# Retention in steps, GpSimd's own stores, SWA's first operands and a new start in an encoder layer

## The chip, the cores and the metric

The kernel runs on one core of a Trainium2 chip. The metric is the device time of one launch in microseconds (us), lower is better. Engines are named as in the profile: PE is TensorE, PEld its weight loads, DVE VectorE, ACT ScalarE, POOL GpSimd, and SP issues most of the transfers. A difference of 0.2% is 4.5 us here.

## The reference

One inference step of a one-layer encoder on 1024 prompt tokens and 64 sample tokens, D_MODEL 1024, all in 32-bit floats. One wide projection gives retention's q, k, v and gate, the queries, keys and values of sliding-window attention (SWA), and two branch gates:

```python
xn = rms_norm(x, g_attn)
rq, rk, rv, rg, sq, sk, sv, ga, gb = split(xn @ w_in)
# A: retention, 4 heads of 256, chunks of 64
q = rope(rq); k = rope(rk) / 16
s = einsum('bihd,bjhd->bhij', q, k) * gamma ** abs(i - j)
o = s @ v + (q @ state) * q_dec
state = state * gamma ** C + (k * k_dec).T @ v
a = (rms_norm(o) * silu(rg)) @ w_ret_out
# B: SWA, 16 heads of 64 on 2 kv heads, window 128, bias by relative position, sinks
p = softmax(sq @ sk.T / 8 + rel_bias, with sinks)
b = (p @ sv) @ w_swa_out
x = x + (sigmoid(ga) * a + sigmoid(gb) * b) @ w_mix_out
x = x + cross_attn(rms_norm(x), memory)      # 4 heads, 256 memory tokens
x = x + (silu(hn @ w_gate) * (hn @ w_up)) @ w_down
return rms_norm(x), states, keys, values
```

The sample part runs the same layer on 64 tokens with cached state, keys and values.

## The kernel before

All 1088 tokens lie along the free axis, in halves of 544. A large product is a Strassen product: one weight matrix of 256 by 1024 is cut into quarters, the sums of quarters P1 to P7 meet the operands B11, T1, T2, B21, T3, B22, T4 and B12, formed once from the tokens. `product` makes one of the seven, `multiply` (L206, L207, L209) issues its 24 matmuls of 128x272 into a PSUM tile `pq`: each 32-bit value is a high and a low part, and three products of parts are added. `split` (L123, L124) makes the parts, the cast on ACT and the remainder on DVE; the sums of weight quarters (L184 to L190) are on POOL. `mm3` (L150 to L152) does the same three-part product for the smaller matmuls. The PSUM results of a Strassen product are combined on DVE (L571) into tiles of a small ring called `stage`, and what is made of them is stored to DRAM.

The order of instructions on each engine comes from a scheduler, which simulates a timeline and takes ready instructions; `tc.high_priority`, `tc.issue_after(x)` and `in_order` steer it.

The stages, by the trace: a start with a first product done in the plain way (`self.plain`) up to 49 us; projections and retention up to about 600; gates and memory to 823; SWA with other products between its steps (`filler`) to about 1035; then merging, cross attention and the feed-forward part, which the change does not touch.

In the start, x is loaded into staging tiles `xr`, multiplied by the gain into `xg` on ACT (L437), and split into operands.

In the projection stage, each head's k, q and v are projected; k and q are rotated with a cosine and sine table `cs`, loaded anew for each half (L603 to L608, the last two additions on POOL), and stored to `d_qkv`. The scheduler mixes the instructions of `retention(h)` among those of the next products. Retention takes blocks of 256 tokens: it loads ks, vf and qs, transposes (`turned`, L702, tile `pk`), computes scores `pss`, the state's update `pkv` and the output `po`; then `ret_out` normalizes `po` into `ret_o` (L816 to L822), turns it by four transposes into `pb` (L826), and stores it. After the four blocks comes the 64-token sample with tiles `psss`, `pos` and `pkvs`.

SWA's queries are stored to `d_sq` in pieces of 256 bytes; the relative bias is read from a table `d_rb` with a stride. SWA's filler first finishes the memory values (`pd` with `wq`, L150; its evictions are L1101), then multiplies retention's result by `w_ret_out` (`ret`, `pd`), whose first operands are loaded from `d_gate` into tiles `swin`, one feature block at a time.

Of the kernel before, what the change touches and what calls it, by code (L numbers as in the profile page):

```python
# [19 lines left out]
P = 128  # L20
# [21 lines left out]
HC = HALF // 2  # L42
OPS = ("B11", "T1", "T2", "B21", "T3", "B22", "T4", "B12")
# [66 lines left out]
class Kernel:  # L110
    def __init__(self, nc, tc, io, decay):
        self.nc, self.tc, self.io, self.decay = nc, tc, io, decay
        self.later = []
        self.refill = None

# [6 lines left out]
    def split(self, src, hi, lo):  # L122
        self.last_cast = self.nc.scalar.copy(hi, src).ins  # L123
        self.nc.vector.tensor_tensor(out=lo, in0=src, in1=hi.bitcast(F32), op=ALU.subtract)  # L124
# [42 lines left out]
    def weight_ops(self, raws, n=512, skip=()):  # L167
# [13 lines left out]
        tt = nc.gpsimd.tensor_tensor  # L181
# [8 lines left out]
        tt(out=a12, in0=a12, in1=a11, op=sub)  # L190
# [21 lines left out]
    def product(self, w, x, name, operand):  # L212
        ps = self.multiply(self.bank_pair(), w[name], x[operand])
# [131 lines left out]
    def run(self):  # L345
        nc, tc, io = self.nc, self.tc, self.io
        with ExitStack() as ctx:
# [27 lines left out]
            self.d_rb = dp.tile([16, 64 * 256], F32, name="d_rb")  # L375

# [4 lines left out]
            with ExitStack() as sctx:  # L381
# [6 lines left out]
                with tc.tile_pool(name="sixth", bufs=1, reuse_waits="tile") as sixth:  # L388
                    self.places = self.places + [sixth]
                    with self.plain_psum(2):  # L390
                        self.mix_phase()
# [23 lines left out]
    def start_phase(self, ctx):  # L415
# [9 lines left out]
        xr = lambda: sp.tile([P, HALF], F32, tag="xr", bufs=4, name="xr")  # L425
        raws = [self.wp.tile([P, 1024], F32, tag="raw", bufs=2, name="raw") for i in range(2)]

        def columns(j):
            for i in range(2):
                self.load(raws[i][:, j * 512:(j + 1) * 512].rearrange("p (k m) -> p k m", m=P), io["w_v"][i][:, 4 * j:4 * j + 4])  # L430

        def pieces(k0, t):
            hs = slice(t * HALF, (t + 1) * HALF)
            for k in range(k0, k0 + 4):
                x = xr()
                self.load(x, io["xT"][k, :, hs])
                nc.scalar.mul(self.xg[k][:, hs], x, g[:, k:k + 1])  # L437

        for n, (k0, t) in enumerate(((0, 0), (0, 1), (4, 0), (4, 1))):
            pieces(k0, t)  # L440
            if n < 2:
                columns(n)
            if n == 1:
                self.operands_early()
        self.load(self.ident, io["c_ident"])
        w = self.plain_weights(raws)
        self.operands_late()
        self.first_sums()
        self.late_sums()
# [15 lines left out]
    def token_roots(self):  # L465
# [4 lines left out]
        for i in range(9):  # L470
            w = P if i < 8 else SMP
            nc.tensor.matmul(pv[:w, i, :], self.rstd[:, i * P:i * P + w], self.ones[:, :2], start=True, stop=True)
# [1219 lines left out]
```

## Time and profile before

| what | value |
|---|---|
| three runs | 2243.85, 2244.88, 2248.97 us; median 2244.88 |
| profiled execution, its time | 2245.5 us |
| its span in the trace | 2243.7 us |
| mean granted clock of TensorE | 0.989 |

The span is what the trace records of that execution; the time beside it is the one measured from outside. In a row of the timeline stand the start, the duration, the engine and line, the operation and its tiles, and in brackets the idle time before it with what ended it. In a row of waits stand the engine and line that waited, what it waited for, and the total, count and longest in us. In a row of instruction groups, after the count, stand the total busy time and the mean of one in ns, then the idle time before. In a row of transfers stand the count, the size and the median time from issue to landing.

### The profile page before, as it was taken

How to read it: one execution, taken by the hardware profiler on the slowest of the kernel's cores; microseconds unless marked ns; L12 is line 12 of the kernel's file. 1: busy time of each engine (PE TensorE's matmuls, PEld its weight loads, DVE VectorE, ACT ScalarE, POOL GpSimd, SP SyncE). 2: the span in 40 equal slices, each digit the busy share in tenths (PEclk: the TensorE clock that was granted, in tenths of full speed). 3: DMA queues.
4: the chain of work that ended last, by engine and by line, in shares of the span. 5: the costliest groups of instructions: out<-in, count | busy, mean ns of one | idle time of the engine just before them, and what ended most of it. 6: DMA issues, size and time to landing. Idle time of an engine off the chain costs nothing.

```text
span 2243.7 us, 42075 instructions
## 1 busy us (share of the span) xinstructions
PE 2164.6 (96%) x16580; PEld 2114.4 (94%) x16580; DVE 1603.1 (71%) x2675; ACT 883.8 (39%) x1902; POOL 703.2 (31%) x471
## 2 busy tenths in 40 slices
PE   7999999999999999999999999999999999999987
PEld 7999998999999987888999998999999999999987
DVE  8986877777687667885455455658777776879777
ACT  7343333345444355554133334333322222335433
POOL 1441533242244112220000000015555565534561
PEclk9999999999999999999999999999999999999999
DMA  5644545443444576326443111422343333376332
GB/s 192 187 134 135 142 138 151 128 137 112 151 145 161 156 227 206 113 82 200 135 153 106 59 48 57 139 88 83 112 140 104 102 107 103 124 248 201 120 119 81
DMA packets 186008, 298.92 MB, mean 133 GB/s; under 512 B 40498, under 2 KB 110034, under 8 KB 185810
## 3 DMA queue, kind: packets, MB, share of 16 engines
q1 hardware_dynamic: 181458, 287.31, 40.9%
q10 hardware_dynamic: 4032, 7.80, 0.9%
q8 instruction: 131, 2.15, 0.4%
q0 software_dynamic: 320, 1.11, 0.1%
q14 instruction: 67, 0.55, 0.1%
HBM read 205.00 MB, written 91.16 MB: 132 GB/s over the span
## 4 chain that ended last, share of the span: by engine, by line
PE 70%; DVE 14%; DMA 7%; issue 3%; POOL 3%; ACT 3%; SPq 0%; POOLq 0%; DVEq 0%; ACTq 0%
PE pq L206 12%; PE pq L209 12%; PE pq L207 12%; PE pd L150 7%; PE pd L152 7%; PE pd L151 7%; DVE wq L124 3%; DVE T L124 1%; DVE B L124 1%; DMA raw<-w_down 1%; PE pss L943 1%; DMA cs<-c_rope 1%; ACT wq L123 1%; DMA hl<-d_op 1%; PE pout L1009 1%
## 5 line engine op out<-in xcount | busy, mean ns | idle before, releaser
L124 DVE TENSOR_TENSOR wq<-raw,wq 128x512 fp32r<-128x512 f32 (+1 forms) x509 | 462.1, 912 | 158.8 <-ACT wq L123 156.6
L123 ACT CAST wq<-raw 128x512 fp32r<-128x512 f32 (+1 forms) x509 | 308.0, 613 | 553.4 <-PE pq L209 206.5
L206 PE MATMUL pq<-T,wq 128*128 128x272 f32 x1832 | 502.8, 292 | 6.8 <-ACT wq L123 5.8
L207 PE MATMUL pq<-T,wq 128*128 128x272 f32 x1832 | 499.0, 289 | 0.0
L206 PE MATMUL pq<-B,wq 128*128 128x272 f32 x1574 | 433.3, 293 | 10.3 <-ACT wq L123 10.2
L207 PE MATMUL pq<-B,wq 128*128 128x272 f32 x1574 | 431.3, 290 | 4.2 <-DVE B L124 4.1
L209 PE MATMUL pq<-T,wq 128*128 128x272 f32 x1832 | 383.3, 289 | 2.5 <-DVE wq L124 2.4
L184 POOL TENSOR_TENSOR raw<-raw 128x512 f32<-128x512 f32 (+1 forms) x59 | 80.8, 1370 | 897.1 <-DVE rs_r L302 487.0
L206 PEld LDWEIGHTS pq<-T,wq 128*128 128x128 f32 x1832 | 346.8, 189 | 8.1 <-ACT wq L123 6.7
L207 PEld LDWEIGHTS pq<-T,wq 128*128 128x128 f32 x1832 | 350.0, 191 | 0.3 <-issue 0.3
L209 PE MATMUL pq<-B,wq 128*128 128x272 f32 x1574 | 329.6, 289 | 0.0
L206 PEld LDWEIGHTS pq<-B,wq 128*128 128x128 f32 x1574 | 298.8, 190 | 11.0 <-ACT wq L123 10.2
L207 PEld LDWEIGHTS pq<-B,wq 128*128 128x128 f32 x1574 | 302.0, 192 | 5.7 <-DVE B L124 5.3
L209 PEld LDWEIGHTS pq<-T,wq 128*128 128x128 f32 x1832 | 286.2, 189 | 3.8 <-DVE wq L124 2.9
L209 PEld LDWEIGHTS pq<-B,wq 128*128 128x128 f32 x1574 | 246.8, 190 | 0.5 <-issue 0.3
L263 DVE TENSOR_TENSOR u<-pq,u 128x544 f32<-128x544 f32 x177 | 127.1, 719 | 76.6 <-PE pq L209 75.9
L187 POOL TENSOR_TENSOR raw<-raw 128x512 f32<-128x512 f32 (+1 forms) x59 | 85.7, 1452 | 120.0 <-DVE wq L124 120.0
L571 DVE TENSOR_TENSOR stage<-pq,u 128x544 f32<-128x544 f32 x112 | 80.3, 717 | 26.0 <-PE pq L209 25.8
L190 POOL TENSOR_TENSOR raw<-raw 128x512 f32<-128x512 f32 (+1 forms) x59 | 90.2, 1529 | 16.0 <-DVE wq L124 12.2
L971 POOL TENSOR_TENSOR t<-t,den 128x768 f32<-128x768 f32 (+2 forms) x34 | 47.6, 1401 | 134.3 <-DVE den L969 56.7
L185 POOL TENSOR_TENSOR raw<-raw 128x512 f32<-128x512 f32 (+1 forms) x59 | 85.5, 1449 | 3.8
L1474 POOL TENSOR_TENSOR y<-u,y 128x544 f32<-128x544 f32 x38 | 61.3, 1628 | 49.3 <-DVE y L1472 24.5
(366 smaller groups left out, 4695.6 us busy)
## 6 DMA issues: line engine op xcount, KB each, us to landing
hl<-d_op SPq DMA_DIRECT2D x84, 272.0 KB, 4.1
d_qkv<-stage SPq DMA_DIRECT2D x44, 272.0 KB, 4.5
d_op<-stage SPq DMA_DIRECT2D x44, 272.0 KB, 2.5
d_op<-ht SPq DMA_DIRECT2D x44, 272.0 KB, 3.8
raw<-w_gate SPq DMA_DIRECT2D x22, 512.0 KB, 3.5
raw<-w_up SPq DMA_DIRECT2D x22, 512.0 KB, 4.2
cs<-c_rope SPq DMA_DIRECT2D x16, 544.0 KB, 4.3
raw<-w_down SPq DMA_DIRECT2D x16, 512.0 KB, 3.9
```

What stands on the lines that cost most here:

```text
L123: self.last_cast = self.nc.scalar.copy(hi, src).ins
L124: self.nc.vector.tensor_tensor(out=lo, in0=src, in1=hi.bitcast(F32), op=ALU.subtract)
L150: mm(ps, wh, xh, start=start, stop=False)
L151: mm(ps, wh, xl, start=False, stop=False)
L152: self.last_mm = mm(ps, wl, xh, start=False, stop=stop).ins
L185: tt(out=a21, in0=a21, in1=a22, op=add)
L187: tt(out=a11, in0=a22, in1=a11, op=sub)
L190: tt(out=a12, in0=a12, in1=a11, op=sub)
L206: mm(ps[:, c, :HC], w[:, 0, ks], x[:, 0, cs], start=start, stop=False)
L207: mm(ps[:, c, :HC], w[:, 0, ks], x[:, 1, cs], start=False, stop=False)
L209: self.last_mm = mm(ps[:, c, :HC], w[:, 1, ks], x[:, 0, c * HC:(c + 1) * HC], start=False, stop=stop).ins
L263: add = lambda out, a, b: nc.vector.tensor_tensor(out=out, in0=a, in1=b, op=ALU.add)
```

## The change

Four pieces of code change together.

1. Start. Twenty matmuls of constants (`WARM`) are put first on PE, and the ACT table is loaded on a constant. x is loaded straight into `xg`; the gain is multiplied into the operands while they are split, high part on ACT and low part on DVE (`put`). The first w_k's sums go to DVE, and the order of T2, T1, T3, T4 is fixed.
2. Retention is written as a generator. After each Strassen product `product` runs one step of it, and PE takes both in program order. Head h's steps run in the products after its own; loads of a block come a step ahead; `ret_out` is cut into `ret_scaled` and `ret_turn`. Head 3's steps run beside the keys, the last queries and three gate products. The rope table is one tile loaded once, and the rope additions of heads 0 and 1 are on DVE.
3. GpSimd issues the stores of what it has computed: retention's q and k for heads 2 and 3, SWA's queries (now rows of 4 KB), SWA's keys and values, gates; and two copies from DRAM to DRAM that lay the bias out in `d_bias`. It issues 59 transfers, 4 before; SP issues 899, 987 before.
4. SWA. PSUM pools are opened in another order; the bias is one load of 128x1536; the first operands of `w_ret_out` come in grouped loads, and their casts stand behind other work; the units of `w_ret_out` are fetched two ahead; queries are loaded two chunks ahead.

The start on ACT, first before and then after: `B` and `b` are Strassen operands, `wq` and `w` weight parts.

```order
L437 ACT_TABLE_LOAD
L437 ACTIVATE xg_112<-xr,gains 128x544 x2
L123 CAST B_157<-xg_112 128x544
L437 ACTIVATE xg_113<-xr,gains 128x544
L123 CAST B_157<-xg_112 128x544
...
L123 CAST wq<-raw 128x512 x2
```

```order
L433 ACT_TABLE_LOAD
L433 ACTIVATE mtok<-ones 128x1
L467 ACTIVATE B_173<-xg_113,gains 128x544
L125 CAST w_185<-raw 128x512
L467 ACTIVATE B_173<-xg_113,gains 128x544
L467 ACTIVATE B_174<-xg_114,gains 128x544 x2
L125 CAST w_187<-raw 128x512
```

The first weight's cast moved from behind seven instructions on tokens to behind one.

Retention on PE: where the result of head 2's first block is turned, before, at a product's end and between the next block's transposes.

```order
L207 MATMUL pq<-T_160,wq 128x272
L209 MATMUL pq<-T_160,wq 128x272 x2
L826 MATMUL pb<-ident,ret_o 128x128 x2
L702 MATMUL pk<-ident,ks 128x128
L826 MATMUL pb<-ident,ret_o 128x128 x2
L702 MATMUL pk<-ident,ks 128x128 x3
L206 MATMUL pq<-T_220,wq 128x272
```

The same kind of place after (head 0's first block), and behind it the end of head 0, where the sample's steps follow one another.

```order
L152 MATMUL pkv<-vb,kt 128x256
L153 MATMUL pkv<-vb,kt 128x256
L154 MATMUL pkv<-vb,kt 128x256
L982 MATMUL pb<-ident,ret_o 128x128 x4
L209 MATMUL pq<-T_175,wq 128x272
```

```order
L154 MATMUL po<-vb,ss 128x256
L823 MATMUL pk<-ident,vf 64x128 x4
L938 MATMUL psss<-qsm,vf 64x64 x2
L982 MATMUL pb<-ident,ret_o 128x128 x4
L947 MATMUL pos<-state,qsm 64x256 x2
L948 MATMUL pos<-kvs,sfs 64x256
L951 MATMUL pkvs<-kvs 128x256 x2
L209 MATMUL pq<-B_173,wq 128x272
```

The turn `pb` moved behind the next block's state update `pkv`, and at head 0's end no Strassen product stands between the steps.

The loads of SWA's start on SP, before and after.

```order
L117 DMA swin_9674<-d_sq 128x4x512
L117 DMA raw<-w_mv 128x1024 x2
L117 DMA swin_9679<-d_gate_80 128x384 x3
L117 DMA swin_9675<-d_rb 64x8x192 x2
L117 DMA swin_9676<-d_gate_80 128x384 x4
L117 DMA raw<-w_mv 128x1024
L117 DMA swin_9676<-d_gate_80 128x384
L117 DMA swin_9678<-d_skv 128x1024
```

```order
L119 DMA swin_9625<-d_sq 128x4x512
L119 DMA raw<-w_mv 128x1024 x2
L119 DMA swin_9626<-d_bias 128x1536
L119 DMA swin_9630<-d_gate_80 128x2x384 x2
L119 DMA swin_9630<-d_gate_80 128x384
L119 DMA swin_9627<-d_gate_80 128x384
L119 DMA swin_9627<-d_gate_80 128x2x384
```

Two strided bias loads became one, ahead of the operands, and the operands' loads are wider.

The diff, cut to its core:

```diff
...
+WARM = 20
...
     def product(self, w, x, name, operand):
-        ps = self.multiply(self.bank_pair(), w[name], x[operand])
+        if self.side is None:
+            ps = self.multiply(self.bank_pair(), w[name], x[operand])
+        else:
+            ps = self.in_order(lambda: self.multiply(self.bank_pair(), w[name], x[operand]))
+            self.in_order(self.step)
         if self.refill is not None:
             self.refill(operand)
...
+        nc.scalar.mul(self.mtok[:, :1], self.ones[:, :1], 1.0)
+        warm = self.norm_psum("warm")
+        for i in range(WARM):
+            nc.tensor.matmul(warm[:, :P], self.ones, self.ones, start=i == 0, stop=i == WARM - 1)
+
+        def rows(k, t):
             hs = slice(t * HALF, (t + 1) * HALF)
-            for k in range(k0, k0 + 4):
-                x = xr()
-                self.load(x, io["xT"][k, :, hs])
-                nc.scalar.mul(self.xg[k][:, hs], x, g[:, k:k + 1])
-
-        for n, (k0, t) in enumerate(((0, 0), (0, 1), (4, 0), (4, 1))):
-            pieces(k0, t)
-            if n < 2:
-                columns(n)
-            if n == 1:
-                self.operands_early()
+            self.load(self.xg[k][:, hs], io["xT"][k, :, hs])
+
+        def columns(i, j):
+            self.load(raws[i][:, j * 512:(j + 1) * 512].rearrange("p (k m) -> p k m", m=P), io["w_v"][i][:, 4 * j:4 * j + 4])
+
+        rows(0, 0)
...
+        def put(name, k, src, g):
+            o = self.ops[name][k]
+            hi = nc.scalar.mul(o[:, 0], src, g).ins
+            return hi, nc.vector.scalar_tensor_tensor(o[:, 1], src, g, o[:, 0].bitcast(F32), ALU.mult, ALU.subtract).ins
+
+        def weight(i, j):
+            self.split(raws[i][:, j * 512:(j + 1) * 512], w[i, j][:, 0], w[i, j][:, 1])
+
+        for n, name in enumerate(("B11", "B12", "B21", "B22")):
+            for k in range(4):
+                behind = put(name, k, qs[k][n], g[:, k + 4 * (n // 2):k + 4 * (n // 2) + 1])
+                if k == 0 and n < 2:
+                    weight(0, n)
+                if k == 2 and n < 2:
+                    weight(1, n)
...
+            self.second = self.weight_ops(self.load_raws([io["w_k"][i] for i in range(2)]), by=nc.vector)
...
+    def bias_rows(self):
+        for e in range(2):
+            src = self.d_rb.rearrange("(p e) c -> e c p", e=2)[e, 63:63 + 64 * 255, :]
+            src = src.rearrange("(i c) p -> i p c", c=255)[:, :, :NKEY]
+            self.nc.gpsimd.dma_start(self.d_bias[e * 64:(e + 1) * 64], src)
...
+                    add = (nc.vector if h < 2 else nc.gpsimd).tensor_tensor
+                    add(out=a, in0=a, in1=sb, op=ALU.subtract)
+                    add(out=b, in0=b, in1=sa, op=ALU.add)
+                    store = self.store if h < 2 else nc.gpsimd.dma_start
+                    store(self.d_qkv[j, 2 * h, :, half(t)], a)
+                    store(self.d_qkv[j, 2 * h + 1, :, half(t)], b)
...
+                    left[t] -= 1
+                    if left[t] == 0:
+                        d = self.d_sq[p].rearrange("p c a q -> p (c a q)")
+                        nc.gpsimd.dma_start(d[:, t * 9 * P:][:, :1024], whole)
+                        nc.gpsimd.dma_start(self.d_sq[p, :, 8, :, t * 32:(t + 1) * 32], part)
...
+            def gate_columns(idx, w, act, m):
+                store = (nc.scalar if idx and (idx, m) != (2, KT - 2) else nc.gpsimd).dma_start
+                put = lambda i, t, o: store(self.d_gate[idx][m + i, :, half(t)], o)
...
+                rope = self.ra.tile([P, 2, T], F32, name="rope")
+                self.load(rope, io["c_rope"])
+                self.out = None
+                rotated(first, 0, 1)
+                with tc.issue_after(self.sums_done):
+                    self.token_squares()
+                self.side = self.retention_begin()
+                rotated(pair("w_q", 0), 0, 0)
+                for h in range(1, H):
+                    rotated(pair("w_k", h), h, 1)
+                    if h == 1:
+                        self.finish_side()
+                        self.side = self.retention_steps(0)
                     rotated(pair("w_q", h), h, 0)
-                    if h == 0:
-                        self.token_roots()
-                        self.retention_setup()
-                    else:
-                        values(pair("w_v", h), h)
-                    if h:
-                        project(pair("w_sq", h - 1), queries(h - 1))
-                    self.retention(h)
-                    if h == 0:
-                        self.spread_roots()
-                    if h == 1:
-                        self.bias_table()
+                    values(pair("w_v", h), h)
+                    queries(pair("w_sq", h - 1), h - 1)
+                    self.finish_side()
+                    self.side = self.retention_steps(h)
+                project(self.load_ops((io["w_sk"], io["w_sv"])), lambda i, t, o: nc.gpsimd.dma_start(self.d_skv[i, :, half(t)], o))
+                with tc.issue_after(self.last_sum):
+                    self.bias_rows()
+                queries(pair("w_sq", 3), 3)
+                for m in (0, 2, 4):
...
+    def step(self):
+        with self.tc.high_priority():
+            return next(self.side, True)
+
+    def finish_side(self):
+        while not self.in_order(self.step):
+            pass
+        self.side = None
+
+    def retention_begin(self):
+        for i in range(6):
+            yield
+        self.token_roots()
+        self.retention_setup()
+        for i in range(3):
+            yield
+        self.spread_roots()
+        yield
+
+    def retention_steps(self, h):
+        yield from self.retention(h)
+        if h == 1:
+            yield
+            self.bias_table()
+        if h == H - 1:
+            for i in range(3):
+                yield
+            self.ret_turn(*self.out)
...
+                             jt == 0 and b == 0, jt == it)
             if b < NBLK - 1:
+                queries = load_queries(b + 1)
                 st = pair("st")
                 self.split(state, st[:, 0], st[:, 1])
-            self.ret_out(h, po, 2 * b, c0, BLK)
-        self.store(io["o_rsp"][h].rearrange("(t p) e -> p t e", p=P), state)
-
-        s0, vf = new("state"), new("vf")
-        kf, qf = (ra.tile([P, 2, SMP], F32, tag=tag, bufs=1, name=tag) for tag in ("sf", "qsm"))
-        self.load(s0, io["cstate"][h].rearrange("(t p) e -> p t e", p=P))
-        vf = vf[:, :, :SMP]
-        for j, x in ((1, kf), (2, vf), (0, qf)):
-            self.load(x, src(j, SEQ, SMP))
+            self.out = self.ret_scaled(h, po, 2 * b, b * BLK, BLK)
...
+            self.po, self.pw = (ctx.enter_context(self.tc.tile_pool(name=n, bufs=1, reuse_waits="tile", space=PSUM))
+                                for n in ("pout", "pw"))
+            ctx.enter_context(self.plain_psum(2))
...
+                if hf == 0 and c % 4 == 2 and c + 2 < 17:
+                    with tc.issue_after(self.last_fetch):
+                        self.load_queries(qTs, c + 2)
...
+            head, (c0, n) = [], CH[0]
+            with tc.high_priority(), tc.issue_after(self.bias_loaded):
+                for t, groups in zip(self.chunk, (((0, 1), (4, 5), (6,)), ((7,), (2, 3)))):
+                    i = 0
+                    for ks in groups:
+                        dst = t[:, i * n:(i + len(ks)) * n].rearrange("p (k c) -> p k c", c=n)
+                        ins = self.load(dst, self.d_gate[0][ks[0]:ks[-1] + 1, :, c0:c0 + n].rearrange("k p c -> p k c"))
+                        head += [(k, dst[:, j]) for j, k in enumerate(ks)]
+                        i += len(ks)
...
+            units = [lambda m=m: self.unit(io["w_ret_out"][m], KT) for m in range(KT)]
+            for m, u, (c0, n) in self.m_major(units, CH, tail=1, lead=2):
...
```

323 lines of the change are left out of this document (202 added, 121 removed).

## The prediction

> **What bounds the kernel now.** I read the page's engine totals first, then the same engines by stage, then TensorE's waits in each stage, and last the timeline around single gaps.
>
> ```profile
> span 2243.7 us, 42075 instructions
> PE 2164.6 (96%) x16580; PEld 2114.4 (94%) x16580; DVE 1603.1 (71%) x2675; ACT 883.8 (39%) x1902; POOL 703.2 (31%) x471
> PE 70%; DVE 14%; DMA 7%; issue 3%; POOL 3%; ACT 3%; SPq 0%; POOLq 0%; DVEq 0%; ACTq 0%
> ```
>
> TensorE is busy 96% of the span and carries 70% of the chain that ended last. Only two kinds of time can be won: TensorE's idle time, and time in which it is counted busy but runs slowly. Busy time and clock by stage show where both lie (the columns are the stage's length, then PE, PEld, DVE, ACT and POOL busy, the granted clock, the DMA share, GB/s):
>
> ```profile
> 0.00:49.00 49.00, 35.09 (x241) 34.20 (x242) 39.32 (x58) 37.07 (x64) 6.53 (x8) 0.97 0.55 179
> 49.00:600.00 551.00, 531.79 (x4142) 519.85 (x4141) 419.53 (x732) 223.93 (x468) 196.73 (x128) 0.98 0.48 143
> 600.00:800.00 200.00, 200.00 (x1610) 200.00 (x1609) 144.18 (x194) 83.55 (x142) 67.97 (x46) 1.00 0.47 151
> 800.00:870.00 70.00, 58.95 (x438) 54.46 (x436) 47.46 (x104) 40.36 (x113) 11.35 (x13) 0.93 0.84 266
> 1650.00:1700.00 50.00, 50.00 (x401) 50.00 (x400) 39.02 (x46) 15.21 (x26) 28.96 (x20) 1.00 0.27 88
> ```
>
> From 600 to 800 and in the late yardstick stage nothing is lost. The yardstick gives the price of one 272-column matmul: 50.00 / 401 = 0.1247 us. Losses lie in the start (0 to 49), in projections and retention (49 to 600) and where sliding-window attention, SWA, begins (800 to 870): the three places that the change touches. What TensorE waited for there, in that order (us in total, times, longest):
>
> ```profile
> PE pq L206 <- ACT wq L123: 10.2, 1, 10.2
> PE pq L207 <- DVE B L124: 3.6, 3, 1.8
> ...
> PE pb L826 <- ACT ret_o L822: 11.3, 7, 4.5
> PE pk L702 <- issue: 2.7, 1, 2.7
> PE pss L150 <- ACT qs L123: 2.2, 1, 2.2
> PE pk L702 <- DMA ks<-d_qkv: 1.9, 1, 1.9
> ...
> PE pd L150 <- ACT wq L123: 2.9, 1, 2.9
> PE pd L150 <- ACT swin L1101: 2.7, 1, 2.7
> PE pd L150 <- DVE stage L571: 2.7, 1, 2.7
> PE pd L920 <- ACT swin L1101: 1.3, 1, 1.3
> PE pout L1009 <- ACT pT L988: 1.2, 1, 1.2
> ```
>
> A wait costs more than itself, as matmul starts around one gap show:
>
> ```profile
> 25.29 0.56 PE L207 MATMUL pq<-B,wq 128*128 128x272 f32 x1 [1.84 <-DVE B L124]
> 25.66 0.43 PE L206 MATMUL pq<-B,wq 128*128 128x272 f32 x1
> 25.88 0.43 PE L207 MATMUL pq<-B,wq 128*128 128x272 f32 x1
> ...
> 29.06 0.28 PE L207 MATMUL pq<-B,wq 128*128 128x272 f32 x1
> 29.19 0.28 PE L206 MATMUL pq<-B,wq 128*128 128x272 f32 x1
> ```
>
> After a gap of 1.84 us the starts stand about 0.22 us apart until about 28.6 and 0.13 apart from 29.06: some 3.3 us at little over half rate, or about 1.5 us lost on top of the gap. The Trainium skill, "TensorE: Matmul & The Clock Gate" (the part on the HAM clock gate), lets the clock drop to half after an idle window of about 3.4 us and rise after as long a busy one. The length of the slow stretch agrees with this row; the idle length does not, 1.84 us being enough here. By the page the shorter waits would cost only themselves, and the sum below would shrink by its slow-clock parts.
>
> **Retention (49 to 600): take 20 us off.** The stage's Strassen matmuls alone (the pq tiles):
>
> ```profile
> 49.00:600.00 551.00, 424.94 (x3158) 0.98 0.48 143
> ```
>
> At the yardstick they need 3158 x 0.1247 = 393.8 us. The other 4142 - 3158 = 984 records are retention and small work; pss, pkv and po are 256 columns wide and their starts stand 0.12 us apart:
>
> ```profile
> 365.27 0.28 PE L152 MATMUL pkv<-vb,kt 128*128 128x256 f32 x1
> 365.39 0.28 PE L150 MATMUL pkv<-vb,kt 128*128 128x256 f32 x1
> ...
> 368.17 0.28 PE L152 MATMUL po<-vb,ss 128*128 128x256 f32 x1
> ...
> 380.23 0.63 PE L826 MATMUL pb<-ident,ret_o 128*128 128x128 f32 x2 [4.49 <-ACT ret_o L822]
> ```
>
> 984 x 0.12 = 118 us, so 512 in all and about 39 of 551 lost. The seven named waits are 11.3 + 2.7 + 2.2 + 1.9 and three of about 0.3, together 19.1. The clock row says 0.98, 2% under full: 551 x 0.02 = 11 us of full-speed work. So about 30 us can be recovered and 9 are not explained. The largest wait has its cause in the last two rows: the output product po ends at 368.2, its normalized result is turned at 380.2, 12 us later, and TensorE has run out of Strassen work 4.5 us before. In the new order the turn (pb) stands four Strassen products after po with the next block's scores and state update between. A product is 24 matmuls, 3.0 us, and beside them stand 8 transposes, 12 score and 12 state matmuls at 0.12: 4 x 3.0 + 32 x 0.12 = 15.8 us against 12. This wait goes. The waits for ks and qs go too, since both are loaded a step or more ahead, and the 16 rope-table loads leave the queue. What is late next: head 0. It has 25 steps for 21 products, so its last four run with nothing between (transposes, sample scores, pb, pos), linked by small operations of VectorE:
>
> ```profile
> L789 DVE TENSOR_SCALAR kvs<-pk,rtok 64x256 f32<-64x256 f32 x4 | 1.9, 472 | 0.2 <-PE pk L702 0.2
> ```
>
> With 0.47 us for each of two or three in a link I estimate 4 us for the links and, as after the gap above, 1.5 for the clock: 5.5. A step that meets a late VectorE stalls too: VectorE is busy 419.53 of 551, 76%, and 16 of GpSimd's rope additions (heads 0 and 1) move to it:
>
> ```profile
> L607 POOL TENSOR_TENSOR stage<-stage,ab 128x544 f32<-128x544 f32 x16 | 28.8, 1799 | 53.0 <-DVE stage L605 42.0 <-DVE rv L819 10.3 <-DVE rs_t L303 0.7
> 15.50 0.72 DVE L124 TENSOR_TENSOR b<-xg,b 128x544 fp32r<-128x544 f32 x1
> ```
>
> 16 x 0.72 = 11.5 us more, hidden as long as 131 us of idle VectorE cover it, and 16 x 1.8 = 29 us less on GpSimd. 30 recoverable less 5.5 for head 0 and some 4 for stalls of single steps is 20. Bounds: nothing (each wait finds a new place) and 30; below nothing is the second rival's matter.
>
> **Start (0 to 49 and the product begun there): take 3 us off.**
>
> ```profile
> 5.35 1.39 ACT L437 ACTIVATE xg<-xr,gains 128x544 f32<-128x544 f32 x2
> ...
> 9.55 1.13 ACT L123 CAST wq<-raw 128x512 fp32r<-128x512 f32 x2
> ...
> 10.22 0.59 PE L206 MATMUL pq<-B,wq 128*128 128x272 f32 x1 [10.22 <-ACT wq L123]
> 10.61 0.43 PE L207 MATMUL pq<-B,wq 128*128 128x272 f32 x1
> ...
> 21.70 1.83 DVE L124 TENSOR_TENSOR T<-xg,T 128x544 fp32r<-128x544 f32 x1
> ```
>
> The first weight's cast stands eighth on ACT before and third now, ahead of it one gained operand of 0.7 us and a table load that no longer waits for data. So the first product can begin near 7.5 instead of 10.2, and the 20 added matmuls on constants fill the wait, so that the slow stretch from 10.22 (0.23 apart) is over by then: another 1.5 to 2.4. But this stage is VectorE's: its 58 operations fill 39.32 us, and the new order gives it all low parts, the combined weights (taken from GpSimd) and the sums, some 68 operations: at the stage's mean of 39.32 / 58 = 0.68 us they need 46, or 44 without two slow ones of before, after 8 more ACT multiplications that it waits for. Starting near 6 with about 5 us of waiting, it ends near 55, about when products 5 to 7 want the last operands. Of the 4 to 5 us won at the front I leave 3; bounds -2 (operands late) and +11 (the whole first wait and all three B waits gone). Less traffic with GpSimd helps: the 1.83 row is one of two sums that took 1.8 instead of 0.72 while GpSimd ran its own.
>
> **SWA's first operands (800 to 870): take 10 us off.** The five waits sum to 10.8 us (11.0 with one of 0.2), and the clock of 0.93 is 70 x 0.07 = 4.9 us: 15.9. The score bank of pd now is one that frees earlier, which removes the wait for stage; the first operand casts stand behind ACT's evictions instead of before them, which removes the two for L1101; the first w_ret_out units are fetched two ahead, for the 2.9. The bias is one contiguous load instead of two scattered ones; its price moves to two DRAM-to-DRAM copies on GpSimd's queue some 200 us earlier, where 31% busy hides them. Late next: the chain score, exponent, transpose of the first chunk (1.2, stays) and one of the others with its clock, 6 us in all. Bounds 0 and 16.
>
> **GpSimd stores its own results: add 3 us.** It issues 4 transfers before and 59 after.
>
> ```profile
> L665 POOL DMA_DIRECT2D d_gate<-stage x4 | 2.3, 584 | 25.0 <-ACT stage L580 25.0
> d_sq<-stage SPq DMA_DIRECT2D x16, 256.0 KB, 3.4
> d_gate<-stage POOLq DMA_DIRECT2D x4, 272.0 KB, 5.5
> ```
>
> 55 x 0.584 = 32 us more for an engine with 1540 idle, and nearly cancelled by the additions that leave it. SP issues 899 transfers where it issued 987, and no longer holds a load behind one of these stores whose data is late; that is what lets the prefetches start. d_sq goes out in 4 KB rows instead of 256-byte pieces. 3 us is taken for stage buffers held longer (5.5 us from issue to landing on GpSimd's queue, 3.4 on SP's); bounds 0 and 32.
>
> **Sum.** -20 - 3 - 10 + 3 = -30. The profiled execution took 2245.5 us, 0.6 over the median of 2244.9; 2245.5 - 30 = 2215.5, and I say 2215.
>
> **Rivals.** (a) VectorE becomes the bound of the retention stage. TensorE now takes steps strictly in their places; each product has 3.0 us for a step whose VectorE part queues behind Strassen's own evictions, at 76% busy. If half the steps' chains overrun by a little, the 20 shrinks to 3: 2245.5 - 13 = 2232. For: the 76%, and the strict order. Against: the old waits were for ACT and DMA, hardly for VectorE.
> (b) The other side: GpSimd's stores block. Each moved issue must find GpSimd free and its data written, and a stage buffer stays taken until then. It decides from 30 / 55 = 0.55 us exposed per store more than taken; if every store holds up its successor by 0.584 and as much again in waiting, 55 x 1.17 = 64 less the 3 taken: 2215.5 + 61 = 2276. For: heads 2 and 3, SWA queries and gates all write through this one queue. Against: 0.584 us and 31% busy. A sentence of the Trainium skill, "SBUF — State Buffer" (the 'DVE blocks DMA' trap), speaks against the change: descriptors written by GpSimd starve while VectorE holds the shared port, some 3.1 us instead of 0.62; by that figure 55 issues cost about 140 us of GpSimd, and the estimate would rise toward this rival. The four issues above, at 0.584 in stages where VectorE is busy 47.46 of 70 and more, don't show it.
> (c) The waits only move: the old scheduler already mixed retention into products, and 19 us of waits find other owners: 2241 to 2250.
> (d) Full recovery: 28 + 6 + 15 = 49: 2197.
>
> **Chances.** Forecast (gain 20 to 42) 0.65; (d) 0.09; (a) 0.14, gain 5 to 20; (c) 0.05; (b) or anything slower 0.07. Faster is 0.65 + 0.09 + 0.14 = 0.88. Within 0.2% (4.5 us, about what repeated runs of this kernel can tell from no change) is 0.05, slower 0.07. A range from 2196 to 2236 leaves out (b), (c), half of (d) and a third of (a): 0.07 + 0.05 + 0.045 + 0.04, about 0.2. Nearly all of it lies on one side, so it needs no second range.
>
> **What would show it.** Right: the pb wait of 11.3 gone from TensorE's waits, projections and retention ending 15 to 25 us earlier, clock 0.99 or 1.00 there, one cluster of waits at head 0's end on psss, pb and pos, first matmul of the plain product near 7.5, the SWA start's five waits down to one or two, GpSimd's issues still near 0.6 us. Wrong: waits of pss or pq for VectorE's qs, ss or u spread over the stage (a); GpSimd issues over 1.2 us with pq waiting for stage buffers (b); a start whose products 5 to 7 wait for T3 or T4 by more than what was won at the front.

## The result and the profile after

The changed kernel took 2262.41 us (median of five runs, 2255.22 to 2263.86), the kernel before beside it 2244.88: a ratio of 1.0068, interval 1.0052 to 1.0083. It is 17.5 us slower by the medians and 0.68% by the ratio, where 30 us faster was predicted. Now and then an execution is far slower whatever the kernel, and such ones are left out of all medians and ratios below, among them one of rcs_swa_undone, of 8800.4 us.

The totals from the page of the changed kernel:

```profile
span 2260.1 us, 42145 instructions
PE 2171.1 (96%) x16620; PEld 2117.7 (94%) x16620; DVE 1596.2 (71%) x2696; ACT 879.3 (39%) x1895; POOL 702.6 (31%) x522
```

The totals tell nothing: every engine is as busy as before. The stages do (same columns as in the prediction):

```profile
0.00:49.00 49.00, 43.89 (x329) 42.69 (x329) 35.62 (x55) 34.43 (x56) 0.20 (x4) 1.00 0.67 235
49.00:600.00 551.00, 510.79 (x3937) 497.31 (x3937) 406.03 (x737) 216.42 (x458) 187.97 (x163) 0.96 0.38 118
600.00:800.00 200.00, 199.98 (x1601) 199.60 (x1601) 146.57 (x195) 81.92 (x139) 80.12 (x64) 1.00 0.49 160
800.00:870.00 70.00, 64.98 (x523) 62.77 (x521) 44.38 (x86) 36.75 (x84) 8.89 (x11) 1.00 0.69 233
```

The start is better (35.09 busy became 43.89). The stage from 49 to 600 is where the time went: TensorE does 3937 records there instead of 4142, at a clock of 0.96 instead of 0.98. SWA's first score came at 843.75 us instead of 823.47, 20.3 later; at the end of the merge the lag was 16.6, so SWA gave back under 4. TensorE's waits in the changed kernel, for 49 to 600 and then for 800 to 900 (`kt` are retention's scaled keys, `sf` its masked scores, `pT` SWA's transposed scores):

```profile
PE pt L525 <- DVE rstd L516: 12.8, 1, 12.8
PE pb L982 <- DVE sf L886: 7.3, 1, 7.3
PE pq L209 <- DVE stage L644: 6.4, 2, 5.7
PE pss L152 <- DVE kt L860: 6.2, 6, 1.9
PE pb L982 <- ACT ret_o L972: 4.3, 1, 4.3
PE pq L209 <- ACT T L125: 3.1, 1, 3.1
...
PE pout L1169 <- ACT pT L1148: 5.5, 1, 5.5
PE pd L152 <- ACT swin L1287: 2.5, 1, 2.5
...
```

The 20.3 us can be taken apart. From the first matmul of a product to SWA's first score, before and then after (length, TensorE busy, clock, DMA share, GB/s):

```profile
10.22:823.47 813.25, 790.35 (x6177) 0.99 0.49 149
7.31:843.75 836.44, 792.16 (x6180) 0.97 0.43 139
```

TensorE's idle time rose from 22.9 to 44.3 us, its busy time by 1.8, and it began 2.9 earlier: 21.4 + 1.8 - 2.9 = 20.3. So it is nearly all waits. The slow clock (the length of each 10 us stretch times what its granted clock lacks to 1) grew from 10.3 to about 22, but it can't be added to them, since part of it lies inside the waits. In the longest wait, in which no matmul ran, the clock was already down:

```profile
90.43:103.20 12.77, 0.00 (x0) 0.62 0.19 61
```

12.77 x 0.38 = 4.9 us of the 22 are in this one wait and cost nothing more. The old waits of this stage are gone, but for one of pb's that now stands at head 0's end. New ones have come, and four places make them.

**The first 105 us.** Engines by stretch, before:

```profile
50.00:105.00 55.00, 50.46 (x378) 49.89 (x377) 51.10 (x86) 21.58 (x38) 26.39 (x16) 0.94 0.60 187
```

and after:

```profile
50.00:105.00 55.00, 35.86 (x256) 35.35 (x256) 52.44 (x74) 19.63 (x33) 11.89 (x8) 0.81 0.37 120
```

VectorE is full from 50 to 105 in both (51 and 52 of 55). Before, TensorE was busy beside it, 50.46 of 55. Now it is busy 35.86. The place is the token roots `pt`, the matmuls that sum the squares of the tokens. VectorE's first and last addition of squares and TensorE's roots, before:

```profile
51.95 0.71 DVE L463 TENSOR_TENSOR rstd<-rstd,xsq 128x544 f32<-128x544 f32 x1
...
83.67 1.88 DVE L463 TENSOR_TENSOR rstd<-rstd,xsq 128x544 f32<-128x544 f32 x1
...
85.83 2.05 PE L472 MATMUL pt<-ones,rstd 128*128 128x2 f32 x18
```

and after:

```profile
60.81 0.71 DVE L516 TENSOR_TENSOR rstd<-rstd,xsq 128x544 f32<-128x544 f32 x1
...
102.44 0.71 DVE L516 TENSOR_TENSOR rstd<-rstd,xsq 128x544 f32<-128x544 f32 x1
...
89.48 0.95 PE L525 MATMUL pt<-ones,rstd 128*128 128x2 f32 x8
...
103.20 1.44 PE L525 MATMUL pt<-ones,rstd 128*128 128x2 f32 x6 [12.77 <-DVE rstd L516]
```

The roots have not moved: in both traces they stand behind 528 matmuls of products, that is behind the plain product and fourteen Strassen products. What they need has moved. The additions began at 51.95 and ended at 85.55, just in time. Now they begin at 60.81, since the change lets them start only behind the last operand's sums (`issue_after(self.sums_done)`), they share VectorE with eight rope additions that were GpSimd's, and they end at 103.15. Which of the two counts for more is not shown. TensorE stands for 12.8 us with products behind the step, and the first of these run at half clock until 110.6.

**Head 0's end.** TensorE's rows of the four steps with nothing between:

```profile
220.71 0.41 PE L823 MATMUL pk<-ident,vf 128*64 128x128 f32 x2 [0.57 <-DVE kvs L932]
221.53 0.45 PE L938 MATMUL psss<-qsm,vf 128*64 128x64 f32 x4 [0.41 <-ACT ret_o L967]
226.29 1.12 PE L982 MATMUL pb<-ident,ret_o 128*128 128x128 f32 x4 [4.31 <-ACT ret_o L972]
227.34 1.97 PE L947 MATMUL pos<-state,qsm 128*64 128x256 f32 x4
...
```

ACT's rows behind the wait of 4.31:

```profile
223.44 0.62 ACT L125 CAST qs<-qs 128x512 fp32r<-128x512 f32 x1 [1.96 <-DMA qs<-d_qkv]
...
225.73 0.91 ACT L972 ACTIVATE ret_o<-ret_o,rr 128x256 f32<-128x256 f32 x2 [1.57 <-DVE rr L316]
```

The normalization that `pb` needs stands on ACT behind a split of the next head's queries, which waits 1.96 us for its load, and then waits 1.57 more for small operations of VectorE.

**The store of d_rb.** GpSimd's and SP's rows around the store of the bias table, the engines and the transfers meanwhile (columns as in the stages above), and then ACT's, VectorE's and TensorE's rows:

```profile
353.42 0.68 POOL L597 DMA_DIRECT2D d_rb<-rb  x1
...
366.79 0.58 POOL L711 DMA_DIRECT2D d_sq<-stage  x1 [9.44 <-issue]
...
357.27 0.34 SPq L119 DMA_DIRECT2D raw<-w_q  x1
...
354.00:366.00 12.00, 12.00 (x99) 12.00 (x98) 4.55 (x9) 3.36 (x7) 3.33 (x5) 1.00 0.90 105
...
371.05 1.14 ACT L125 CAST wq<-raw 128x512 fp32r<-128x512 f32 x2 [9.17 <-DMA raw<-w_q]
...
371.70 0.69 DVE L126 TENSOR_TENSOR wq<-raw,wq 128x512 fp32r<-128x512 f32 x1 [8.23 <-ACT wq L125]
374.36 0.72 DVE L644 TENSOR_TENSOR stage<-pq,u 128x544 f32<-128x544 f32 x1 [1.96 <-DMA d_sq<-stage]
...
378.07 0.73 DVE L886 SCALAR_TENSOR_TENSOR sf<-pss,rtok,dm 128x256 f32<-128x256 f32 x2
...
378.94 0.44 PE L982 MATMUL pb<-ident,ret_o 64*128 64x64 f32 x2 [7.35 <-DVE sf L886]
```

The 1 MB store is issued in 0.68 us and takes 13.1 to land. It reads the table from 16 partitions, and while it moves the DMA engines are 90% busy with 105 GB/s. One pair of d_sq stores follows at once; the next stands 9.44 us with nothing shown that it waits for. But SP's load of w_q, issued 3.9 us behind the store, is late as well: it takes 13.7 us, where 5.0 is the median of these loads. So VectorE waits first 8.23 us behind those weights and then 1.96 for a stage tile that d_sq frees late; sf stands behind both, and TensorE waits 7.35 us.

The kernel before had this store too, from SP at 351.60. Its largest wait (4.49 us at 380.23) also came behind it, and 9 us earlier ACT had stood for the load of retention's keys:

```profile
371.21 0.62 ACT L123 CAST ks<-ks 128x512 fp32r<-128x512 f32 x1 [4.60 <-DMA ks<-d_qkv]
```

How much of that wait the store made is not shown.

**SWA's second chunk.** ACT's and TensorE's rows:

```profile
871.23 2.96 ACT L125 CAST ret<-swin 128x320 fp32r<-128x320 f32 x8
874.10 0.58 ACT L1148 COPY pT<-pp 64x512 f32<-64x512 f32 x1
...
874.72 1.12 PE L1169 MATMUL pout<-pT,swin 64*64 64x128 f32 x8 [5.49 <-ACT pT L1148]
```

The casts that no longer stand ahead of one eviction stand ahead of another copy. A run below shows that they are only part of this wait.

### The profile page after: what moved, and what is told of

Read it like the earlier page. It is cut to its first block, busy times and chain, and to the rows that moved or that the text cites. A ratio compares the mean times of both kernels' runs of the same rounds, so it can differ in the third digit from the quotient of the medians.

```text
span 2260.1 us, 42145 instructions
## 1 busy us (share of the span) xinstructions
PE 2171.1 (96%) x16620; PEld 2117.7 (94%) x16620; DVE 1596.2 (71%) x2696; ACT 879.3 (39%) x1895; POOL 702.6 (31%) x522
## 4 chain that ended last, share of the span: by engine, by line
PE 73%; DVE 12%; DMA 5%; issue 4%; ACT 3%; POOL 3%; SPq 0%; POOLq 0%; DVEq 0%; ACTq 0%
PE pq L209 14%; PE pq L212 14%; PE pq L210 14%; PE pd L152 7%; PE pd L153 7%; PE pd L154 7%; DVE wq L126 2%; DMA hl<-d_op 1%; DVE T L126 1%; PE pss L1103 1%; DVE B L126 1%; PE pout L1169 1%; DVE stage L644 1%; DVE u L270 1%; PE pp L1146 1%
## 5 line engine op out<-in xcount | busy, mean ns | idle before, releaser
L209 PE MATMUL pq<-B,wq 128*128 128x272 f32 x1526 | 419.9, 293 | 0.7 <-DVE stage L644 0.6
L210 PE MATMUL pq<-B,wq 128*128 128x272 f32 x1526 | 415.7, 289 | 0.6 <-DVE B L126 0.5
L186 POOL TENSOR_TENSOR raw<-raw 128x512 f32<-128x512 f32 (+1 forms) x58 | 78.7, 1357 | 962.5 <-DVE rs_r L309 486.0
L212 PE MATMUL pq<-B,wq 128*128 128x272 f32 x1526 | 317.0, 288 | 0.0
L210 PEld LDWEIGHTS pq<-B,wq 128*128 128x128 f32 x1526 | 291.9, 191 | 1.0 <-DVE B L126 1.0
L209 PEld LDWEIGHTS pq<-B,wq 128*128 128x128 f32 x1526 | 289.0, 189 | 1.8 <-DVE stage L644 0.9
L212 PEld LDWEIGHTS pq<-B,wq 128*128 128x128 f32 x1526 | 238.2, 189 | 0.0
L189 POOL TENSOR_TENSOR raw<-raw 128x512 f32<-128x512 f32 (+1 forms) x58 | 82.7, 1426 | 122.1 <-DVE wq L126 122.1
L193 POOL TENSOR_TENSOR raw<-raw 128x512 f32<-128x512 f32 (+1 forms) x58 | 88.5, 1527 | 15.7 <-DVE wq L126 12.2
L187 POOL TENSOR_TENSOR raw<-raw 128x512 f32<-128x512 f32 (+1 forms) x58 | 85.3, 1471 | 3.7
L1661 POOL TENSOR_TENSOR y<-u,y 128x544 f32<-128x544 f32 x38 | 61.4, 1632 | 49.6 <-DVE y L1659 29.2
```

The source lines that it names most:

```text
L187: tt(out=a21, in0=a21, in1=a22, op=add)
L193: self.last_sum = tt(out=a12, in0=a12, in1=a11, op=sub).ins
L209: mm(ps[:, c, :HC], w[:, 0, ks], x[:, 0, cs], start=start, stop=False)
L210: mm(ps[:, c, :HC], w[:, 0, ks], x[:, 1, cs], start=False, stop=False)
L212: self.last_mm = mm(ps[:, c, :HC], w[:, 1, ks], x[:, 0, c * HC:(c + 1) * HC], start=False, stop=stop).ins
```

## The experiments

All ratios are to the kernel before on the same chip. The runs were made on several chips, on which the kernel before had medians from 2243.78 to 2246.80 us, so a difference of a few us between medians is no more than a hint, and the ratio decides.

| run | median us | ratio, interval |
|---|---|---|
| changed kernel | 2262.41 | 1.0068 (1.0052 to 1.0083) |
| start_undone | 2262.58 | 1.0087 (1.0071 to 1.0103) |
| swa_undone | 2259.12 | 1.0073 (1.0058 to 1.0088) |
| retention_undone | 2245.74 | 1.0010 (1.0001 to 1.0020) |
| roots_late | 2251.38 | 1.0040 (1.0027 to 1.0053) |
| r_squares | 2256.22 | 1.0048 (1.0033 to 1.0063) |
| r_rb_sp | 2250.39 | 1.0010 (0.9997 to 1.0023) |
| r_stores_sp | 2247.13 | 1.0002 (0.9993 to 1.0012) |
| chain_alone | 2241.69 | 0.9981 (0.9971 to 0.9990) |
| r_chain | 2232.47 | 0.9941 (0.9927 to 0.9956) |
| rc_swafix | 2234.51 | 0.9948 (0.9932 to 0.9964) |
| rc_nowarm | 2242.28 | 0.9986 (0.9975 to 0.9997) |
| rc_stores_sp | 2226.83 | 0.9913 (0.9891 to 0.9934) |
| rcs_start_undone | 2227.74 | 0.9929 (0.9912 to 0.9947) |
| rcs_swa_undone | 2227.65 | 0.9926 (0.9901 to 0.9951) |
| rcs_squares_late | 2227.41 | 0.9926 (0.9906 to 0.9947) |

**Which part loses: undo one at a time.** start_undone puts back `start_phase`, swa_undone `mix_phase`, `swa` and `filler`, retention_undone `project_phase`, `retention` and `ret_out`.

> The changed kernel with the start of the kernel before (no warm matmuls, gain on ACT into xg, T sums by the old order); steps, GpSimd's stores and SWA as changed. Theory A (the loss is made by VectorE's full first 105 us, in which TensorE waits at fixed places: 3.1 for T, 5.7 for stage, 12.8 for the token roots, with half clock after each): with the old start the squares of the tokens begin about 4 us earlier and VectorE has fewer operations, so the roots' wait falls to 8 or less and the run to 2250 to 2257 us, against 2262 changed. Theory B (GpSimd's stores hold stage tiles and cause the loss): nothing of it is in the start, so the run is slower by what the start won, 2265 to 2270. Theory C (the strict step order costs it all over the retention stage): 2262 to 2268.

> The changed kernel with SWA's part as before (bias read by a stride, old pools, operands and casts, no copies of the bias). From the traces: TensorE stood 20.3 us behind at SWA's first score and 16.6 behind at the last product of the merge, so SWA's part won about 3.5 us: theory A and C expect 2264 to 2268 us. Theory B expects less than the changed kernel, 2255 to 2260, as the two copies of the bias leave GpSimd's queue.

> The start and SWA as changed, but projections and retention as before: the scheduler mixes retention, SP and ACT store, the rope table is loaded in halves, and the bias is copied once to its new layout. All theories put the loss into steps or stores, so this must be faster than before: SWA 3.5 us, start 3 us, 2236 to 2242 us. If it is 2250 or more, the new start by itself makes the loss, whatever the order behind it.

Measured: 2262.58, 2259.12 and 2245.74. The loss sits in the steps and stores: without them it is gone. But the start and SWA alone are no faster than before (1.0010), where the prediction had taken 13 us off for them. start_undone did not come out as theory A said: the old start moves some waits (6.6 instead of 12.8 at the token roots) and brings back its own (a first matmul at 11.4 and three waits for B), and the sum is not better. Its additions of squares run from 61.4 to about 101.6 us, as late as with the new start. swa_undone came out in theory B's range by the median, but its ratio is not different from the changed kernel's, and its first score came 4 us later, not earlier, so it does not speak for theory B.

**The token roots.**

```diff
     def retention_begin(self):
-        for i in range(6):
+        for i in range(10):
             yield
         self.token_roots()
```

> The changed kernel with the matmuls of the token roots four Strassen products later in the list of steps (after ten products instead of six). Theory A: the wait of 12.8 us for the squares and the half clock after it go, four products being 12 us: 2246 to 2251 us. Theory B and C, or A with VectorE's backlog only met elsewhere: 2258 to 2263.

Measured 2251.38, 11 us less than the changed kernel by the medians and 6 by the ratios; in the traces SWA's first score comes 10.5 us earlier. Of its waits, 49 to 600, these belong to the roots:

```profile
PE pb L536 <- DVE rtok L312: 1.8, 1, 1.8
PE pt L525 <- DVE rstd L516: 1.6, 1, 1.6
```

12.8 us became 1.6, and another 1.8 further on. One number in the list of steps is worth a good part of the loss.

**GpSimd's queue, head 0's end, VectorE's load**, all with the roots late. r_rb_sp and r_stores_sp replace `nc.gpsimd.dma_start` by `self.store`, for d_rb alone or for the stores of stage tiles. r_squares puts the 14 additions in `token_squares` on GpSimd. r_chain lets steps run on:

```diff
-                    self.finish_side()
-                    self.side = self.retention_steps(h)
+                    self.side = chain(self.side, self.retention_steps(h))
```

> With the token roots four products later (2251.4 us) and the one store of the bias table d_rb issued by SP instead of GpSimd. In the trace of the changed kernel GpSimd stood 9.4 us with nothing to wait for behind that store, the next d_sq store went out late, a stage tile came free late, VectorE's evictions slipped and TensorE waited 7.3 us for pb behind VectorE's sf. Theory A with this chain: 7 to 9 us off, 2242 to 2245. If VectorE's backlog alone makes that wait: no change, 2249 to 2253.

> With the token roots four products later and all stores of stage tiles (d_qkv, d_sq, d_skv, d_gate) back on SP; d_rb and the two copies of the bias stay on GpSimd. Theory A: only the wait behind d_rb can go, 2242 to 2247. Theory B (each of GpSimd's stores costs the path something): 2235 to 2240. If SP's queue now holds loads behind stores: 2250 or more.

> With the token roots four products later and the steps of one head running on into the next head's products, so that head 0's last four steps no longer stand back to back (all steps of later heads move back by as many). The changed kernel waited there 4.3 for pb and about 3 in smaller gaps, with a clock of 0.66 in those 10 us: theory A expects 6 to 8 us off, 2243 to 2246. Theory C (a strict order costs at every step, wherever it stands): 2249 to 2253.

> With the token roots four products later, the 14 additions of squared tokens on GpSimd instead of VectorE, and the squares behind the last operand's cast on ACT (two waits named). Theory A: 14 x 0.64 = 9 us leave VectorE where it is full, and the casts of T3 no longer stand behind three squares: the waits of 3.3 for T and 5.0 for stage shrink, 5 to 9 us off, 2242 to 2246. If GpSimd's additions collide with VectorE's (1.8 us instead of 0.72 in the trace): 2250 or more.

r_chain: 2232.47, 19 us less than roots_late (22 by the ratios), far more than the 6 to 8 expected, and faster than before. Its waits from 125 to 816 us are nearly all of this (TensorE's clock is 1.00 there):

```profile
PE pss L153 <- DVE kt L860: 4.5, 3, 2.5
PE po L153 <- DVE state L902: 2.8, 2, 2.6
PE pq L210 <- DVE stage L645: 1.8, 1, 1.8
...
```

Both clusters are gone. Head 0's end is spread over products. The 7.3 us wait went too: in the new order the weights w_q are loaded at 341.43 us, ahead of the store of d_rb at 344.58. Up to SWA's first score TensorE's idle time fell from 36.3 to 24.7 us and its busy time from 797.0 to 791.4.

r_rb_sp gives no clear answer in time: its median is within 1 us of roots_late, its ratio 0.3% lower. Its trace tells more. SP issues the store at 343.32, as early as GpSimd did in roots_late, GpSimd no longer stands behind it, and still VectorE and ACT wait (their rows):

```profile
360.92 0.72 DVE L644 TENSOR_TENSOR stage<-pq,u 128x544 f32<-128x544 f32 x1 [5.77 <-DMA d_sq<-stage]
...
361.56 1.14 ACT L125 CAST wq<-raw 128x512 fp32r<-128x512 f32 x2 [6.53 <-DMA raw<-w_q]
```

So it is the transfer that holds the others up, whichever queue it stands in, and not GpSimd's queue alone. TensorE's 7.3 is 0.6, and 1.4 for stage and 3.7 for a later kt have come in its place. A store of the table that doesn't read from 16 partitions was not tried.

r_stores_sp: about 4 us less than roots_late (8 by the ratios), at the upper end of theory A's range. In its trace the 7.3 is gone and the waits for kt are 8.9 instead of 5.9. r_squares brought nothing: 5 us slower by the medians, with ratios that overlap. The wait for T went, but TensorE waited 2.4 and 2.7 for VectorE's weight parts instead, since the additions took about 1.8 us each on GpSimd and its sums for the next weights stood behind them.

**Alone, and together.**

> The changed kernel with only the heads' steps running on into the next head's products; the token roots stay where the change put them. With the roots late as well this gave 2232.5 us against 2251.4 without. If the two losses are separate: 2262.4 - 19 = 2243.5, give or take 3. If the steps that run on only help once the roots are late: 2250 or more.

> Roots late, steps running on, and the stores of stage tiles back on SP. If GpSimd's own stores cost little but for the wait behind d_rb, which fell from 7.3 to about 2 us of TensorE's time there: 2229 to 2233. If each store has a price (theory B): 2225 or less. If GpSimd's stores help: 2235 or more.

> Roots late, steps running on, and in SWA the casts of the second and third chunk of w_ret_out's operands placed behind ACT's last copy of transposed scores (pT) instead of behind the last exponent. In the trace eight such casts, 2.96 us, stood ahead of the pT copy that TensorE waited 5.16 us for. If that wait is made by this order: 3 to 6 us off 2232.5, so 2226 to 2230. If the wait only moves to the next operand or weight: 2231 to 2234.

> Roots late, steps running on, and one matmul of constants at the start instead of 20. The first real matmuls should then run at half rate for some 3 us, as before. If what is won at the front is given back at the waits for T and stage (TensorE stood 9.7 us ahead at the 240th product and 3 behind at the 360th): no change, 2231 to 2234. If it counts: 2 us slower, 2234 to 2236.

chain_alone, 2241.69: the two losses are separate, 20.7 us and, with the roots, about 9 more. rc_stores_sp, 2226.83: with the stage stores off GpSimd some 6 us less (the intervals 0.9891 to 0.9934 and 0.9927 to 0.9956 touch), though d_rb stays on GpSimd; in its trace the waits for kt are 1.5 instead of 4.5, and why is open. rc_swafix (casts behind the pT copy) shortened the wait for pT from 5.2 to 3.9 and that for swin from 2.8 to 1.3, and the time stayed. So those casts make only part of the wait for pT; ACT still had a weight load to wait for (1.73 us) and other casts ahead of the copy. rc_nowarm was wrong in my forecast: it is 8 us slower than rc_swafix beside it. In its trace TensorE stands 2.4 us behind r_chain at the 240th matmul of products, 3.9 at the 360th and 4.1 at SWA's first score; the other half of the 8 is not in the trace of that one execution and stays open.

**What the start and SWA are worth without those waits.**

> Roots late, steps running on, stores on SP (2226.8 us), and the start of the kernel before. Tells what the new start is worth once the waits behind it are gone. In the trace the old start under the new order reached the 528th Strassen matmul 4.6 us later than the new one. If that counts: 2229 to 2232. If the start's win is absorbed by VectorE: 2225 to 2228. My prediction's term: 3 us, 2230.

> Roots late, steps running on, stores on SP, and SWA's part as before. My prediction's term for the new SWA part was 10 us: 2237. By the traces its waits and its slow clock went from 20.9 us to 16.7 and a new wait for pT came: 2227 to 2231. If it does nothing: 2225 to 2228.

> Roots late, steps running on, stores on SP, and the squares of the tokens behind the last operand's cast on ACT too (before, only their additions stood behind the last sum). In the trace a run of squares stood ahead of T3's casts on ACT and TensorE waited 3.0 us for T. If that order makes the wait: 2 to 5 us off, 2222 to 2225. If VectorE's sums behind it are the bound: 2226 to 2229, with the same time lost at stage.

2227.74, 2227.65 and 2227.41 against 2226.83, with intervals that overlap: the new start and SWA's new part are worth 1 us each, and none of them differs from nothing. So the 8 us of rc_nowarm are not what the whole new start is worth: the old start, which has no warm matmuls either, is as fast here. rcs_squares_late shows how such a win is lost. TensorE's waits up to 126 us in rc_stores_sp:

```profile
PE pq L210 <- DVE stage L645: 4.8, 1, 4.8
PE pq L210 <- ACT T L126: 3.0, 1, 3.0
PE pb L537 <- DVE rtok L313: 1.8, 1, 1.8
PE pt L526 <- DVE rstd L517: 1.6, 1, 1.6
```

and in rcs_squares_late, where the squares stand behind the last operand's cast:

```profile
PE pt L526 <- DVE rstd L517: 6.8, 1, 6.8
PE pq L210 <- DVE stage L645: 3.5, 1, 3.5
PE pq L210 <- DVE u L271: 2.3, 1, 2.3
```

7.8 us of waits for T and stage became 5.8 for stage and u, and the token roots took 5.2 more. VectorE has a fixed load up to 105 us; what TensorE doesn't wait for early it waits for late.

rc_stores_sp, with the roots late, steps running on and stage tiles stored by SP, is the best: 0.87% below the kernel before (0.66 to 1.09), about 36 us below the changed one.

## Why the prediction was wrong, point by point

- **Retention, 20 us off: the step that failed is "hidden as long as 131 us of idle VectorE cover it", and with it "30 recoverable less 5.5 for head 0 and some 4 for stalls of single steps".** The old waits did go, as argued. But VectorE's idle time was counted over 551 us, and from 50 to 105 it had only 4 (51.10 of 55 busy before). In this stretch the moved rope additions and the later squares met, the last square was added 17.6 us later, and the token roots, a step whose operands I never asked for, waited 12.8 us; roots_late got 6 to 11 us of the loss back. I had worked out that VectorE ends its start work near 55 and stopped there; the last operand's split ran until 60.9, and rope and 14 additions of squares until 103.
- **The transfers, put at nothing.** The sum has no term for one transfer that holds up another. The store of d_rb, 13.1 us long, made the weights of w_q and a stage tile late and cost TensorE 7.35 us. The largest old wait was read as an order of instructions alone, and it too came behind this store.
- **Head 0's end, 5.5 us: mechanism right, too small.** Its waits were 4.3 and about 1, where 4 stood for the links; but the normalization behind a load of queries made one link of 4.3. The gain of r_chain and chain_alone, 19 to 21 us, also holds the pile-up behind d_rb, and the two are parted by the traces only.
- **The clock.** The prediction counted 11 us of slow clock as recoverable, from a clock row of two digits; finer stretches give 8.5 for that stage. Up to SWA it grew from 10 to 22, but what it cost beside the waits grew by about 2 us, as TensorE's busy time did. Rival (a) was the nearest of the rivals in its cause, VectorE late at fixed places, but its price of 17 lost from the 20 was too low, since it spoke of half the steps a little late, and it was few steps by much.
- **Start, 3 us off: the front's part right, the whole nearly nothing.** First matmul at 7.31 (7.5 forecast), 9.8 us ahead at the 240th matmul of products, 3.2 behind at the 360th. The bound of -2 was the better value. (The bound of +11 is less than the 10.2 and 3.6 us of waits that it names.)
- **SWA, 10 us off: mis-sized.** Between the first score and the merge TensorE's idle time fell from 15.6 to 13.7 us and its busy time by 1.8, 3.7 in all. I had allowed 1.2 for pT and one other wait. pT alone took 5.5, in part behind the operand casts that were moved ahead of it. Undoing SWA's part changed the ratio by 0.05% and 0.13% in two runs, neither clear of nothing.
- **GpSimd, 3 us on: sign right, measured about 6, cause not shown.** Issues averaged 0.55 to 0.73 us by group, as forecast; rival (b) as priced, 1.17 us for every one, did not occur. The 6 us came without moving d_rb, so the one big store does not explain them.

The Trainium skill's page "SBUF — State Buffer" (the 'DVE blocks DMA' trap) speaks of 3.1 us instead of 0.62 for a GpSimd transfer beside a VectorE copy. No issue here came near it: the 59 took 0.54 to 0.74 us. But 661 of VectorE's 736 computing instructions from 49 to 600 us are TENSOR_TENSOR or SCALAR_TENSOR_TENSOR and only 23 are copies, so this case hardly tests that rule, and it should not have been read as speaking of any busy VectorE.

## What to carry to other kernels

When work that a scheduler could place freely becomes a step at a fixed place on the busiest engine, list every step, not only the long chain it was meant for, and ask of each when its last operand is ready on the other engines. Do it stretch by stretch: 131 us of idle time over a stage were 4 us where they were needed. Let the steps of one unit run on into the next instead of draining them, since a drained list runs with nothing between. And before you credit an earlier start or a moved cast, look at what the supplying engine has left to do: if it is full, the wait moves and the sum stays. Look, too, at what moves on the DMA engines when a load is issued: one slow store made a weight load take 13.7 us.

## What the runs showed of the hardware that was not expected

- A 1 MB store read from 16 partitions (d_rb, 13.1 us to landing) held the DMA engines 90% busy with 105 GB/s in the changed kernel (354 to 366 us), and 80% with 117 GB/s in the kernel before (352 to 365). What was issued behind it was late on both kinds of queue: a load of SP took 13.7 us, and GpSimd's second pair of stores stood 9.44 us before it was issued. GpSimd also stood after the copies of the bias: 3.36 and 1.89 us.
- The granted clock falls inside a long wait and not only behind it: 0.62 in the 12.77 us up to 103.20, in which no matmul ran.
- Twenty matmuls of constants ahead of the first real one were worth 2.4 us by the 240th matmul in the trace and about 8 us in the runs, and half of the 8 stays open.
